# Engine order in the mixers of a two-layer hybrid encoder, and VectorE instead of GpSimd for the first weight's low half

## The chip, the cores and the metric

The kernel runs on one core of a Trainium2 chip. The metric is device time in microseconds for one launch, the median of the runs; lower is better. Engines are named as in the profile: PE is TensorE's matmul stream and PEld its weight loads, DVE is VectorE, ACT ScalarE, POOL GpSimd, SP SyncE, whose queue issues most DMAs here.

## What is computed

The input x is 512 x 1024 in fp32, the whole trunk is fp32, and the output must agree with an fp32 reference:

```python
for layer in range(2):
    h = rmsnorm(x, norm_mix[layer])
    if layer % 2 == 0:   # DeltaNet (4 heads of 128, both directions) | dilated windows (8 heads of 64)
        mixed = mixer_ab(h, ab_w_in, conv_w, a_log, dt_bias, norm_w, ab_w_out)
    else:                # retention (4 heads) | Hyena (long convolution through an FFT)
        mixed = mixer_cd(h, cd_w_in, log_decay, ..., cd_w_out)
    x = x + mixed
    x = x + conv_ffn(rmsnorm(x, norm_ffn[layer]), ffn_w_in, ffn_conv_w, ffn_conv_b, ffn_w_out)
return rmsnorm(x, final_norm)
# in DeltaNet: beta = sigmoid(b); g = -exp(a_log) * softplus(a + dt_bias)
#   sol = triangular_solve(I + strict(k_beta k^T * decay), [v * beta, k_beta * exp(g)])
```

## The kernel before

**Projections.** Every big product is done as three matmuls in a reduced fp32 format: each operand is split into a high and a low half (`whi`, `wlo`, `hh`, `hl`, ...), and `mm3` (L262 to L267) adds high by high, high by low and low by high. `fetch` (L240) takes a loaded weight block `raw` (128 x 1024 numbers, three buffers), lets ScalarE write `whi` (L253) and VectorE write `wlo` = raw - whi (L254). With `pool_lo` set, GpSimd does L254 instead. `get(ahead)` fetches until `ahead` blocks are ready and hands out the oldest; four ready blocks have room (`WB`). Activations are split in the same way by `split` (L225 on ScalarE, L226 on VectorE).

**What sets the order.** Each engine works through its own queue in order. In `start` (L189) the order is that of the program (`manual_schedule`). Everywhere else a list scheduler at build time orders each queue: by its own cost model it picks, of what it believes to be ready, what stands first in the program. `tc.issue_after(ins)` adds one constraint: what is traced in the block on `ins`'s engine comes behind `ins` in that queue; other engines are not bound by it.

**Start.** The four row tiles of x are squared and summed (L128, ScalarE), the power is taken on GpSimd (L129, L130), `scale` (L139, VectorE, two halves of a tile) multiplies by it and by the norm's row, and `turn` (L152 and the split) transposes to `hh` and `hl`. Tiles 0 and 1 come first, with the first weight block between; then tiles 2 and 3 with a block each. `first` (L278) then projects three column blocks, first over tiles 0 and 1, then over 2 and 3. `pool_lo` stays set after `start`, so the fourth block, fetched in `first`, has its low half made by GpSimd in either kernel.

**Layer 0, dilated attention, gates, DeltaNet.** `dilated` runs 16 units (scores, softmax, transposes `tp` copied to `pT` at L539, product `op` at L548), three deep. At the units named in `DPROJ` it also projects, and the last two entries call the generator `gates`: at the first it multiplies out the gate columns, at the second it computes beta and g in some 20 small operations on VectorE and ScalarE (L618 to L653), Exp at L631 and L639, Ln at L634 and L642. The third call comes in the first tile of `delta_prep` and holds the cumulative sums (`gp`, L659). `delta_prep` projects q, k and v (`tile`, each with the short convolution `conv3`, whose two VectorE steps L366 and L367 read and then release the projection's accumulator), and the gate Z (`proj_tok`). `deltanet` then inverts the triangular blocks: `Bt` is transposed (L851), 30 rank-one steps follow on VectorE (L858, L859), two transposes (L864, L865), products of 32 x 32 blocks `m32` (L890) copied to `T32` (L892), diagonal copies into P (L895), products `m32b` (L900) copied into P (L902), then the same with 64 x 64 blocks (`vp` L912, copies L913, L921, L923, L930, L932), and last a scan over four chunks. Eight units of the output projection (`fill`, 12 matmuls `oacc` each) are strewn between by `FILLS` to give PE work; `wb` are their four weight blocks.

**Layer 1.** `retention` projects q and k in four column blocks (three in `first`, one as `rqk`). Each is moved out of its accumulator by ScalarE (`rope_in`, L458), half-rotated by four DMAs (L460) and finished in `rope_out` (L467 to L478), with ScalarE casts at L474. The accumulators are then taken by `proj_tok` (`pt`). `hyena` projects 12 column blocks `hap`; after the eighth-part `HT` of the matmuls of a block it transposes u (`tp`, L1240).

Of the kernel before, what the change touches and what calls it, by code (L numbers as in the profile page):

```python
# [15 lines left out]
S = 512  # L16
# [47 lines left out]
def bc(ap, shape):  # L64
    return ap.to_broadcast(shape)
# [97 lines left out]
class K:  # L163
# [26 lines left out]
    def start(self, n):  # L190

        self.x = self.new_x()
        for what in (0, 1, None, None, 2, None, 3):
            self.load_w() if what is None else self.load_x(what)
        n.spread()
        self.warm_up(WARM)
        n.whole(0)
        n.scale(0)
        n.whole(1)
        n.scale(1)  # L200
        self.pool_lo = True
        self.fetch()
        self.pool_lo = False
        for g in range(2):
            for t in range(2):
                n.turn(t, (g,))
        for t in range(2, 4):
            self.fetch()
            n.whole(t)
            n.scale(t)  # L210
        self.pool_lo = True
# [146 lines left out]
    def conv3(self, out, ps, w, o, b=None):  # L358

        nc = self.nc  # L360
        w0, w1, w2 = [w[:, k:k + 1] for k in o]
        if b is None:
            nc.scalar.activation(out, ps, AF.Copy, scale=w1)
        else:
            nc.scalar.activation(out, ps, AF.Identity, scale=w1, bias=b)
        nc.vector.scalar_tensor_tensor(out[:, 1:], ps[:, :S - 1], w0, out[:, 1:], op0=ALU.mult, op1=ALU.add)  # L366
        nc.vector.scalar_tensor_tensor(out[:, :S - 1], ps[:, 1:], w2, out[:, :S - 1], op0=ALU.mult, op1=ALU.add)  # L367

# [233 lines left out]
    def gates(self, dp, n):  # L602
# [29 lines left out]
        V.tensor_scalar(e, e, 1.0, None, op0=ALU.add)  # L632
        nl = T("gnl")
        nc.scalar.activation(nl, e, AF.Ln)  # L634
        V.reciprocal(beta, e)
        V.tensor_tensor(y, gt[:, :, 8:16], bc(row[:, 0:1, :], [128, 4, 8]), op=ALU.add)
        V.tensor_scalar(u, y, -1.0, None, op0=ALU.mult)
        V.tensor_tensor(u, u, y, op=ALU.min)
        nc.scalar.activation(e, u, AF.Exp)  # L639
        nc.scalar.activation(row[:, 1, :], row[:, 1, :], AF.Exp)  # L640
        V.tensor_scalar(u, e, 1.0, None, op0=ALU.add)
        nc.scalar.activation(g, u, AF.Ln)  # L642
        V.tensor_scalar(u, u, -1.0, None, op0=ALU.add)
        V.tensor_scalar(g2, u, 0.0, None, op0=ALU.is_equal)
# [7 lines left out]
        V.tensor_tensor(g, g, y, op=ALU.add)  # L652
        V.scalar_tensor_tensor(g, g, -1.0, bc(row[:, 1:2, :], [128, 4, 8]), op0=ALU.mult, op1=ALU.mult)  # L653
        yield
        gp = self.wk((128, 128), "gp")
# [48 lines left out]
    def delta_prep(self, dp, n, gates, K_, Q_, V_, Z_):  # L704
# [24 lines left out]
        def tile(which, h):  # L729
            f = which * 4 + h  # L730
            ap = self.acc(nm="ap")
            self.last_ap = self.proj_t(self.get(), n, ap).ins
            next(gates, None)
            c = self.vscr.pop(0) if which == 2 else self.s2("c")
            self.conv3(c, ap, cw, (f, 12 + f, 24 + f))
            if which < 2 or h == 0:
                nc.scalar.activation(c, c, AF.Silu)
            pend.append((c, which, h))
# [26 lines left out]
    def deltanet(self, n, gates, yb, nxt):  # L765
        nc, I = self.nc, self.I
        V = nc.vector
        with ExitStack() as ctx:
# [81 lines left out]
            Xf = X.rearrange("p a b -> p (a b)")  # L850
            V.transpose(Xf, Bt.rearrange("p m s -> p s m"))  # L851
            tm = dp.tile([128, 256], F32, name="tm")
# [14 lines left out]
            for t in range(NT):  # L867
                self.load_x(t)
            wb = [self.get() for _ in range(4)]
            units = [(t, half) for half in range(2) for t in range(NT)]  # L870
# [17 lines left out]
            for m in range(16):  # L888
                for (d, s, o), p in zip(pairs, ps):
                    nc.tensor.matmul(p[blk(o), m, :], P[d][blk(s), m, blk(o)], Yv[d][blk(s), :, 16 * d + m], start=True, stop=True, tile_position=(32 * s, 32 * o))  # L890
            for i, ((d, s, o), p) in enumerate(zip(pairs, ps)):
                (V.tensor_copy if i % 2 else nc.scalar.copy)(T32[blk(o)], p[blk(o)])  # L892
            for q in range(4):
                for d in range(2):
                    (V.tensor_copy, nc.scalar.copy)[d](P[d][blk(q), :, blk(q)], Yu[d][blk(q), :, 16 * d:16 * d + 16].rearrange("p a m -> p m a"))  # L895
            fill(FILLS[1])
            ps = [self.wk((128, 16, 32), "m32b") for _ in pairs]
            for m in range(16):
                for (d, s, o), p in zip(pairs, ps):
                    nc.tensor.matmul(p[blk(s), m, :], T32[blk(o), m, :], Yu[d][blk(o), :, 16 * d + m], start=True, stop=True, tile_position=(32 * o, 32 * s))  # L900
            for i, ((d, s, o), p) in enumerate(zip(pairs, ps)):
                (V.tensor_copy if i % 2 else nc.scalar.copy)(P[d][blk(s), :, blk(o)], p[blk(s)])  # L902
            fill(FILLS[2])
# [124 lines left out]
    def retention(self, n, order):  # L1028
        nc, I = self.nc, self.I
        V = nc.vector  # L1030
        with ExitStack() as ctx:
# [12 lines left out]
            for i in range(4):  # L1044
                if i == 3:
                    self.proj_t(self.get(), n, ps[3])
                rin.append(self.rope_in(rp, ps[i], 1.0 if i // 2 else 0.125, self.rope_room() if i % 2 else None))
                if i < 2:
                    rot(i)
            with self.tc.issue_after(rin[3][2].ins):  # L1050
                rot(2)
                rot(3)
            v = rp.tile([128, NT, 512], F32, name="rv")
# [278 lines left out]
TPD = lambda k: k.acc  # L1332
DPROJ = (0, 2, 5, 8, 10, 15)
DAT = (1, 2)
# [5 lines left out]
IA = 3  # L1340
HT = 6
HSKIP = (1, 3)
# [58 lines left out]
```

## Time and profile before

| | |
|---|---|
| median of 3 runs | 1330.83 us (1330.3 to 1331.14) |
| the profiled execution | 1330.02 us, its span 1328.2 us |
| PE busy | 1304.8 us, 98% of the span |
| DVE, ACT, POOL busy | 750.6, 531.6, 147.4 us |
| mean granted TensorE clock | 0.996 |
| DMA | 123.61 MB, 31.2% of the 16 engines' time |

The page is read from the top: a busy time near the span names the engine that sets the end, and what that engine waits for (the waits, by who ended them) is what an edit can win. Where it is busy all the time but at a lower granted clock, the stretch table (busy time by engine, granted clock, DMA) shows it. The timelines give start, duration, engine, line, operation and, in brackets, how long the engine had stood idle and who ended that.

### The profile page before, as it was taken

How to read it: one execution, taken by the hardware profiler on the slowest of the kernel's cores; microseconds unless marked ns; L12 is line 12 of the kernel's file. 1: busy time of each engine (PE TensorE's matmuls, PEld its weight loads, DVE VectorE, ACT ScalarE, POOL GpSimd, SP SyncE). 2: the span in 40 equal slices, each digit the busy share in tenths (PEclk: the TensorE clock that was granted, in tenths of full speed). 3: DMA queues.
4: the chain of work that ended last, by engine and by line, in shares of the span. 5: the costliest groups of instructions: out<-in, count | busy, mean ns of one | idle time of the engine just before them, and what ended most of it. 6: DMA issues, size and time to landing. Idle time of an engine off the chain costs nothing.

```text
span 1328.2 us, 17628 instructions
## 1 busy us (share of the span) xinstructions
PE 1304.8 (98%) x6977; PEld 1093.2 (82%) x6977; DVE 750.6 (57%) x1085; ACT 531.6 (40%) x840; POOL 147.4 (11%) x176
## 2 busy tenths in 40 slices
PE   7999999999999999999999999999999999999997
PEld 6877788878988888888889787888898888888886
DVE  6777559957754433444436837869754442244432
ACT  4566648344433331233326424442443331133332
POOL 3354120003000000000001200124100000000002
PEclk9999999989999999999999999999999999999999
DMA  7531113411333333333323513330243333333321
GB/s 219 129 94 36 51 32 96 143 49 60 93 113 96 95 95 95 96 95 97 98 91 101 162 48 92 102 94 18 67 140 95 95 95 96 87 117 98 95 79 64
DMA packets 161025, 123.61 MB, mean 93 GB/s; under 512 B 6985, under 2 KB 134477, under 8 KB 160944
## 3 DMA queue, kind: packets, MB, share of 16 engines
q1 hardware_dynamic: 160798, 122.43, 31.2%
q8 instruction: 55, 0.90, 0.3%
q14 instruction: 26, 0.21, 0.1%
q10 hardware_dynamic: 146, 0.07, 0.0%
HBM read 117.23 MB, written 2.10 MB: 90 GB/s over the span
## 4 chain that ended last, share of the span: by engine, by line
PE 84%; DVE 7%; ACT 4%; issue 2%; DMA 1%; POOL 1%; SPq 0%; POOLq 0%; ACTq 0%; DVEq 0%
PE gup L266 11%; PE gup L265 11%; PE gup L267 11%; PE oacc L265 7%; PE oacc L267 7%; PE oacc L266 7%; PE hap L267 2%; PE pt L265 2%; PE hap L265 2%; PE hap L266 2%; PE pt L267 2%; PE pt L266 2%; PE ap L267 1%; PE ap L265 1%; PE ap L266 1%
## 5 line engine op out<-in xcount | busy, mean ns | idle before, releaser
L254 DVE TENSOR_TENSOR wlo<-raw,whi 128x1024 fp32r<-128x1024 f32 x191 | 236.0, 1237 | 304.1 <-ACT whi L253 299.3
L253 ACT CAST whi<-raw 128x1024 fp32r<-128x1024 f32 (+1 forms) x197 | 206.7, 1050 | 427.6 <-PE gup L266 186.8
L265 PE MATMUL gup<-hh,whi 128*128 128x512 f32 x656 | 255.2, 389 | 0.0
L266 PE MATMUL gup<-hl,whi 128*128 128x512 f32 x656 | 255.2, 389 | 0.0
L267 PE MATMUL gup<-hh,wlo 128*128 128x512 f32 x656 | 255.2, 389 | 0.0
L267 PEld LDWEIGHTS gup<-hh,wlo 128*128 128x128 f32 x656 | 123.1, 188 | 25.6
L265 PEld LDWEIGHTS gup<-hh,whi 128*128 128x128 f32 x656 | 123.2, 188 | 25.6
L266 PEld LDWEIGHTS gup<-hl,whi 128*128 128x128 f32 x656 | 123.2, 188 | 25.4
L265 PE MATMUL oacc<-whi,ghi 128*128 128x512 f32 x352 | 137.1, 389 | 0.0
L267 PE MATMUL oacc<-whi,glo 128*128 128x512 f32 x352 | 137.0, 389 | 0.0
L266 PE MATMUL oacc<-wlo,ghi 128*128 128x512 f32 x352 | 136.9, 389 | 0.0
L267 PEld LDWEIGHTS oacc<-whi,glo 128*128 128x128 f32 x352 | 66.1, 188 | 13.7
L265 PEld LDWEIGHTS oacc<-whi,ghi 128*128 128x128 f32 x352 | 66.1, 188 | 13.7
L266 PEld LDWEIGHTS oacc<-wlo,ghi 128*128 128x128 f32 x352 | 66.1, 188 | 13.6
L430 DVE TENSOR_TENSOR sl<-gup,sl 128x512 f32<-128x512 f32 x42 | 29.0, 692 | 81.8 <-PE gup L267 81.8
L315 DVE TENSOR_TENSOR x<-oacc,x 128x512 f32<-128x512 f32 x64 | 43.4, 685 | 49.3 <-PE oacc L267 49.2
L429 ACT ACTIVATE sl<-c 128x512 f32<-128x512 f32 x44 | 27.8, 632 | 89.2 <-DVE c L367 89.2
L265 PE MATMUL first<-hh,whi 128*128 128x256 f32 x192 | 54.9, 288 | 0.0
L266 PE MATMUL first<-hl,whi 128*128 128x256 f32 x192 | 54.5, 284 | 0.2 <-DVE hl L226 0.2
L267 PE MATMUL first<-hh,wlo 128*128 128x256 f32 x192 | 54.3, 283 | 0.0
L265 PE MATMUL pt<-whi,hh 128*128 128x512 f32 x128 | 50.2, 392 | 2.6 <-ACT room L458 1.7
L104 POOL TENSOR_SCALAR ss<-ss 128x1 f32<-128x1 f32 x16 | 5.0, 312 | 429.3 <-ACT jk L102 429.3
(422 smaller groups left out, 2346.4 us busy)
## 6 DMA issues: line engine op xcount, KB each, us to landing
raw<-in_ffn_w_in_dram SPq DMA_DIRECT2D x88, 512.0 KB, 3.8
raw<-in_ffn_w_out_dram SPq DMA_DIRECT2D x44, 512.0 KB, 3.9
raw<-in_ab_w_in_dram SPq DMA_DIRECT2D x28, 512.0 KB, 3.9
raw<-in_cd_w_in_dram SPq DMA_DIRECT2D x24, 512.0 KB, 4.3
x<-in_x_dram SPq DMA_DIRECT2D x16, 256.0 KB, 5.0
raw<-in_ab_w_out_dram SPq DMA_DIRECT2D x8, 512.0 KB, 3.8
raw<-in_cd_w_out_dram SPq DMA_DIRECT2D x8, 512.0 KB, 3.8
rs<-rt SPq DMA_DIRECT2D x32, 64.0 KB, 2.0
```

What stands on the lines that cost most here:

```text
L104: nc.gpsimd.tensor_scalar(ss[:, 1:2], ss[:, 0:1], s, EPS, op0=ALU.add, op1=ALU.add)
L253: self.nc.scalar.copy(hi, raw)
L254: (self.nc.gpsimd if self.pool_lo else self.nc.vector).tensor_tensor(lo, raw, hi, op=ALU.subtract)
L265: mm(out, a[0], b[0], start=start, stop=False)
L266: mm(out, a[0], b[1], start=False, stop=False)
L267: return mm(out, a[1], b[0], start=False, stop=stop)
L315: self.nc.vector.tensor_add(xs, acc, xs)
L429: nc.scalar.activation(sl, c, AF.Silu)
L430: nc.vector.tensor_mul(sl, up, sl)
```

## The change

There are seven edits. (1) In `start` the first block's low half is made by VectorE, in its program place behind the scaling of tile 1. (2) In `gates` the Ln for the key gate works on a copy and stands behind the other Ln, the second call comes at unit 18 rather than 15, and there is one more empty stop before the cumulative sums, so that these come a projection tile later. (3) `conv3` returns its last instruction, and the transpose L851 is queued behind that of the last tile. (4) The last of the four `get` calls for `wb` fetches nothing ahead. (5) The diagonal copies into P are queued behind the `T32` copies, six on VectorE and two on ScalarE rather than four and four, and two blocks are fetched behind the `m32b` copies. (6) In `retention` `rope_out` of block 1 is traced behind block 3's `rope_in`, its ScalarE part queued behind that. (7) `HT` goes from 6 to 7.

```diff
@@ start
-        self.pool_lo = True
         self.fetch()
-        self.pool_lo = False
@@ conv3
-        nc.vector.scalar_tensor_tensor(out[:, :S - 1], ps[:, 1:], w2, out[:, :S - 1], op0=ALU.mult, op1=ALU.add)
+        return nc.vector.scalar_tensor_tensor(out[:, :S - 1], ps[:, 1:], w2, out[:, :S - 1], op0=ALU.mult, op1=ALU.add)
@@ gates
-        nl = T("gnl")
-        nc.scalar.activation(nl, e, AF.Ln)
         V.reciprocal(beta, e)
 ...
         V.tensor_tensor(u, u, y, op=ALU.min)
+        nl = T("gnl")
+        V.tensor_copy(nl, e)
         nc.scalar.activation(e, u, AF.Exp)
         nc.scalar.activation(row[:, 1, :], row[:, 1, :], AF.Exp)
         V.tensor_scalar(u, e, 1.0, None, op0=ALU.add)
         nc.scalar.activation(g, u, AF.Ln)
+        nc.scalar.activation(nl, nl, AF.Ln)
 ...
+        yield
         yield
         gp = self.wk((128, 128), "gp")
@@ delta_prep
-            self.conv3(c, ap, cw, (f, 12 + f, 24 + f))
+            self.last_conv = self.conv3(c, ap, cw, (f, 12 + f, 24 + f)).ins
@@ deltanet
-            V.transpose(Xf, Bt.rearrange("p m s -> p s m"))
+            with self.tc.issue_after(self.last_conv):
+                V.transpose(Xf, Bt.rearrange("p m s -> p s m"))
 ...
-            wb = [self.get() for _ in range(4)]
+            wb = [self.get(1 + (i < 3)) for i in range(4)]
 ...
-            for i, ((d, s, o), p) in enumerate(zip(pairs, ps)):
-                (V.tensor_copy if i % 2 else nc.scalar.copy)(T32[blk(o)], p[blk(o)])
-            for q in range(4):
-                for d in range(2):
-                    (V.tensor_copy, nc.scalar.copy)[d](P[d][blk(q), :, blk(q)], Yu[d]...)
+            out = [(V.tensor_copy if i % 2 else nc.scalar.copy)(T32[blk(o)], p[blk(o)]).ins
+                   for i, ((d, s, o), p) in enumerate(zip(pairs, ps))]
+            with self.tc.issue_after(out[2]), self.tc.issue_after(out[3]):
+                for q in range(4):
+                    for d in range(2):
+                        (nc.scalar.copy if d and q % 2 else V.tensor_copy)(P[d][blk(q), :, blk(q)], Yu[d]...)
 ...   (the m32b copies likewise become a list `out`)
+            with self.tc.issue_after(out[2]), self.tc.issue_after(out[3]):
+                for _ in range(2):
+                    self.fetch()
@@ retention
-                if i < 2:
+                if i == 0:
+                    rot(0)
+            with self.tc.issue_after(rin[3][2].ins):
+                for i in range(1, 4):
                     rot(i)
-            with self.tc.issue_after(rin[3][2].ins):
-                rot(2)
-                rot(3)
@@
-DPROJ = (0, 2, 5, 8, 10, 15)
+DPROJ = (0, 2, 5, 8, 10, 18)
-HT = 6
+HT = 7
```

## Rows read from the trace of the kernel before

**Rows 1.** Waits of PE, whole span: who, released by, total us, times, longest.

```profile
PE m32b L900 <- DVE s L892: 1.9, 2, 1.4
...
PE pt L265 <- ACT room L458: 1.7, 1, 1.7
...
PE m32b L900 <- ACT s L892: 1.2, 1, 1.2
...
PE pt L265 <- DVE scr L367: 0.9, 1, 0.9
...
PE op L548 <- ACT pT L539: 0.9, 1, 0.9
...
PE tp L1240 <- ACT hsh L225: 0.6, 1, 0.6
```

**Rows 2.** Timeline of the start, 8 to 28 us: start, us, engine, line, operation, [idle].

```profile
8.29 1.41 DVE L139 SCALAR_TENSOR_TENSOR xn<-x,ss,nrow 128x512 f32<-128x512 f32 x2
...
10.08 2.35 POOL L254 TENSOR_TENSOR wlo<-raw,whi 128x1024 fp32r<-128x1024 f32 x1
...
10.16 3.48 DVE L139 SCALAR_TENSOR_TENSOR xn<-x,ss,nrow 128x512 f32<-128x512 f32 x2 [0.46 <-POOL ss L130]
...
13.03 2.82 PE L152 MATMUL nt<-ident,xn 128*128 128x128 f32 x12 [2.83 <-DVE xn L139]
...
14.80 0.69 DVE L226 TENSOR_TENSOR hl<-nt,hh 128x512 fp32r<-128x512 f32 x1 [0.56 <-ACT hh L225]
...
15.87 0.41 PE L266 MATMUL first<-hl,whi 128*128 128x256 f32 x1
...
16.24 0.28 PE L265 MATMUL first<-hh,whi 128*128 128x256 f32 x1
...
22.48 3.54 DVE L139 SCALAR_TENSOR_TENSOR xn<-x,ss,nrow 128x512 f32<-128x512 f32 x2 [0.46 <-POOL ss L130]
...
27.87 0.39 PE L266 MATMUL first<-hl,whi 128*128 128x256 f32 x1 [0.21 <-DVE hl L226]
```

**Rows 3.** Timeline of ACT at the end of the dilated units, 134 to 138 us.

```profile
134.39 1.28 ACT L634 ACT_TABLE_LOAD   x1
...
137.36 0.57 ACT L539 COPY pT<-tp 128x512 f32<-128x512 f32 x1
...
137.94 1.28 ACT L642 ACT_TABLE_LOAD   x1
```

**Rows 4.** Timeline of DVE at the end of the projections, 228 to 232 us.

```profile
228.91 2.06 DVE L851 STREAM_TRANSPOSE L<-Bt 128x1024 f32<-128x1024 f32 x1
...
230.90 0.71 DVE L367 SCALAR_TENSOR_TENSOR scr<-ap,dncw,scr 128x511 f32<-128x511 f32 x1
```

**Rows 5.** Timeline of DVE in the block inverse, 262 to 276 us.

```profile
262.43 1.21 DVE L865 STREAM_TRANSPOSE vs<-L 128x1024 f32<-128x1024 f32 x1
...
266.02 1.28 DVE L251 SCALAR_TENSOR_TENSOR wlo<-raw,dnw,whi 128x1024 fp32r<-128x1024 f32 x1 [0.71 <-ACT whi L250]
...
267.92 1.26 DVE L895 COPY P<-vs 32x512 f32<-32x512 f32 x2
...
271.12 1.42 DVE L892 COPY s<-m 32x512 f32<-32x512 f32 x2
...
274.58 1.42 DVE L902 COPY P<-m32b 32x512 f32<-32x512 f32 x2 [1.32 <-PE m32b L900]
```

**Rows 6.** Timeline of ACT and of PE there: first `T32` copies, output unit.

```profile
269.52 1.18 ACT L892 COPY s<-m 32x512 f32<-32x512 f32 x2
...
265.90 0.50 PE L265 MATMUL oacc<-whi,yh 128*128 128x512 f32 x1
```

**Rows 7.** Stretches: width, busy us by engine (instructions), PEclk, DMA share, GB/s.

```profile
235.00:264.00 29.00, 29.00 (x133) 23.73 (x132) 27.45 (x62) 6.91 (x10) 1.04 (x1) 1.00 0.47 155
...
272.17:279.00 6.83, 6.41 (x147) 4.67 (x148) 2.53 (x5) 1.54 (x4) 1.04 (x1) 0.50 0.47 156
```

**Rows 8.** Timeline of ACT in retention, around 740 us.

```profile
740.18 0.60 ACT L458 ACTIVATE room<-rqk 128x512 f32<-128x512 f32 x1
```

More of the change, by code (lines that the diff above doesn't have):

```diff
@@ L890, in deltanet @@
                     nc.tensor.matmul(p[blk(o), m, :], P[d][blk(s), m, blk(o)], Yv[d][blk(s), :, 16 * d + m], start=True, stop=True, tile_position=(32 * s, 32 * o))
-            for i, ((d, s, o), p) in enumerate(zip(pairs, ps)):
-                (V.tensor_copy if i % 2 else nc.scalar.copy)(T32[blk(o)], p[blk(o)])
-            for q in range(4):
-                for d in range(2):
-                    (V.tensor_copy, nc.scalar.copy)[d](P[d][blk(q), :, blk(q)], Yu[d][blk(q), :, 16 * d:16 * d + 16].rearrange("p a m -> p m a"))
+            out = [(V.tensor_copy if i % 2 else nc.scalar.copy)(T32[blk(o)], p[blk(o)]).ins
[3 more added lines that the diff above has]
+                    for d in range(2):
+                        (nc.scalar.copy if d and q % 2 else V.tensor_copy)(P[d][blk(q), :, blk(q)], Yu[d][blk(q), :, 16 * d:16 * d + 16].rearrange("p a m -> p m a"))
             fill(FILLS[1])
@@ L900, in deltanet @@
                     nc.tensor.matmul(p[blk(s), m, :], T32[blk(o), m, :], Yu[d][blk(o), :, 16 * d + m], start=True, stop=True, tile_position=(32 * o, 32 * s))
-            for i, ((d, s, o), p) in enumerate(zip(pairs, ps)):
-                (V.tensor_copy if i % 2 else nc.scalar.copy)(P[d][blk(s), :, blk(o)], p[blk(s)])
+            out = [(V.tensor_copy if i % 2 else nc.scalar.copy)(P[d][blk(s), :, blk(o)], p[blk(s)]).ins
+                   for i, ((d, s, o), p) in enumerate(zip(pairs, ps))]
+            with self.tc.issue_after(out[2]), self.tc.issue_after(out[3]):
+                for _ in range(2):
+                    self.fetch()
             fill(FILLS[2])
```

## The prediction

> **What bounds the kernel now.** The page's busy times come first: PE works 1304.8 of the span's 1328.2 us, so PE sets the end; DVE, the next, works 750.6. What an edit can win lies in the 23.4 us in which PE does not work, and in stretches in which it works at the lower clock. So I read the waits of PE next. The six that the mixers' edits can touch are [rows 1]: 1.9 and 1.2 us at the block inverse (one place, two releasers), 1.7 in retention, two of 0.9 in layer 0, 0.6 in hyena, 7.2 us in all. The seventh stands in the timeline of the start: PE waits 2.83 us for the scaling of tile 1 [rows 2]. Last, the stretch table shows the one place where the clock fell inside the kernel: for 6.83 us from 272.17 PE ran at 0.50, the 1.2 GHz level, while the stretch up to 264 has 1.00, the 2.4 GHz level [rows 7]. It fell after PE had waited at the block inverse, so that place costs more than its waits. The sum is made against the profiled execution (1330.02 us, 1.8 of it outside the span); the median of the runs lies 0.8 above it, which I add at the end.
>
> **1, the start.** Two scaling steps of tile 0 take 1.41 us; those of tile 1 take 3.48, while GpSimd makes the low half from 10.08 for 2.35 us [rows 2]. The difference, 2.07 us, goes with the GpSimd operation: that ends at 12.43, and the transposes that need the first half of tile 1 start at 13.03. The Trainium skill, SBUF — State Buffer, section "Who interferes with whom", says that a VectorE operation with two SBUF inputs and a GpSimd operation that reads SBUF do not share but block each other for a whole operation; by that, too, the gain is the blocked time, and nothing changes for tile 3, whose scaling takes 3.54 us at 22.48 [rows 2] beside the fourth block's low half, which stays on GpSimd.
>
> What is added: VectorE makes the low half itself, 1.28 us if I take the scaled form [rows 5] for it, ahead of the splits in its queue. Scaling then ends at 11.6, the low half at 12.9, the first `hl` (0.69) at 13.6, the second at 14.3. Before, the second ended at 15.49 (14.80 + 0.69) after an idle 0.56 that now vanishes [rows 2]. So the projection starts 2.07 - 1.28 + 0.56 = 1.35 us earlier. Two corrections. A matmul takes 0.41 us at 15.87 and 0.28 at 16.24, two further on [rows 2], which is where the clock rises; if it rises no sooner, 1.3 us at one matmul every 0.19 are seven more at the lower level, 0.13 x 7 = 0.9 us lost. On the other side the second half of `first` begins at 27.87 on a `hl` that stands behind the scaling of tile 3 [rows 2], and this chain moves by up to 2.07, as ScalarE's splits do. Gain 1.5 us, bounds 0.4 and 2.1.
>
> **2, the gates.** Three table loads, the first at 134.39 and the last at 137.94, 1.28 us each, stand in ScalarE's queue among the last softmax copies; a `pT` copy comes at 137.36 behind two of them [rows 3], and PE waits 0.9 us for it [rows 1]. With the second call at the last unit these operations are traced behind the last product, and with both Ln together one load serves in place of three. The cover is then the first projection tile and the next, 24 matmuls each; the empty stop moves `gp` behind the second, so the chain has two tiles' time instead of one. Gain 0.9. Bounds 0.9 and -0.4: four small transposes now stand at the very end of the units, where a late copy of the gate columns would hold PE; the nearest row for such a stall is the 0.6 wait for one ScalarE copy [rows 1], of which I take most. The Trainium skill, ScalarE: Activation LUTs, "Table sets: the hidden batching unit", names a set that holds both exp and ln; by it the new order of the Ln would save no load. The three loads of the rows say that the program does not use such a set.
>
> **3, the transpose L851.** It takes 2.06 us at 228.91, in front of L367 at 230.90 [rows 4]; L367 frees the accumulator for which PE waits 0.9 us [rows 1]. Put behind, L367 comes 2 us earlier and that wait goes. But VectorE is busy 27.45 of the 29 us up to 264 [rows 7], with the steps that end in L865 at 263.64 [rows 5] and so release `m32`; swapping two of its operations does not shorten that chain. PE comes 0.9 earlier and waits there. I count nothing, bounds 0 and 0.9 (the upper, if the planner draws another output unit ahead of `m32`).
>
> **4 and 5, the block inverse.** Now both queues do diagonal copies (1.26 for two on VectorE) and two scaled splits (1.28 each on VectorE [rows 5]) before the four `T32` copies, which come at 269.52 on ScalarE [rows 6] and at 271.12 on VectorE, 1.42 for two [rows 5]. `m32` has ended by 265.90, where an output unit begins [rows 6]; the last `T32` copy ends at 272.54, and 3.1 us of PE's time before that are waits [rows 1], so the unit covers PE to about 269. After: `T32` right behind `m32`, done by 265.9 + 1.4 = 267.3, inside the unit; `m32b` can start at 269 instead of 272.5. The 3.1 us of waits go. If the clock then stays up, the 6.41 us of PE work at 0.50 [rows 7] shrink as well, by 3.2 if all of it streams, which the small products do not.
>
> Against that: VectorE has six diagonal copies (6 x 0.63 = 3.8) and some three additions of output units (0.69 each, as the `hl` step of the same size [rows 2]; 2.1) in front of its two `m32b` copies, so these end near 267.3 + 3.8 + 2.1 + 1.4 = 274.6, and `vp` needs them. `m32b` took 2.0 (272.54 to 274.58 [rows 5]) and ends at 271; one output unit of 3 us is all that PE has from there. Behind come the two splits, 2.56 on VectorE and about that on ScalarE, in front of the copies of `vp`; until now both engines had done them earlier. Before, the `m32b` copies ended at 276.0 (274.58 + 1.42). So the path is 1.4 us shorter at that point, 3.1 if the planner puts those copies sooner, and part of the 3.2 of the clock comes on top. I take 2.9, nearer to the upper of these two than to the sum of everything. Bounds 0.5 (the splits take the rest) and 6.3 (3.1 + 3.2).
>
> **6, retention.** `rqk` is moved out at 740.18 [rows 8], behind the casts of block 1 in ScalarE's queue, and PE waits 1.7 us for its accumulator [rows 1]. The copy takes 0.60 and its input is ready before block 1's casts are; queued first it needs to come only 1.7 sooner. What it delays are casts whose readers come after the four weight blocks of `pt`. Gain 1.7, bounds 0.8 (it still stands behind the casts of block 0 and a split) and 1.7.
>
> **7, hyena.** The transposes of u stand three matmuls later, each at least 0.19 after the one before (those of 256 columns, [rows 2]; these have 512), and the wait was 0.6 [rows 1]. Gain 0.6, bounds 0 (the last u's splits then reach the forward transform later) and 0.6.
>
> **The sum.** 1.5 + 0.9 + 0 + 2.9 + 1.7 + 0.6 = 7.6 us: 1330.0 - 7.6 = 1322.4 for a profiled execution, 1323.2 for the median. Low bounds: 0.4 - 0.4 + 0 + 0.5 + 0.8 + 0 = 1.3; high: 2.1 + 0.9 + 0.9 + 6.3 + 1.7 + 0.6 = 12.5. Neither end is likely on all seven at once, so I take 2.0 and 11.5 off the median: 1319.3 to 1328.8.
>
> **Rivals.**
> A, the wait moves on in the block inverse: PE waits for `vp`'s copies behind the two splits, the clock falls as before, and edits 3 to 5 bring nothing. For it: one unit of 3 us must cover 3.6 (271 to 274.6) and the splits. Against: 3.1 us of wait go at the outset. Time: 1323.2 + 2.9 = 1326.1.
> B, PE's gains are waited away in layer 0: chains on VectorE and ScalarE set the pace there, and what the start and edits 2 to 5 give is given back; retention and hyena stay. Time: 1330.8 - 2.3 = 1328.5, no change by measure. For it: VectorE hardly pauses before 264 [rows 7]. Against: these chains begin on what PE delivers, so they move with it.
> C, the order does not come out as meant: the planner goes by its own times, and nothing binds VectorE in edit 6 or ScalarE in edit 2. Then a wait of about the same size stands beside each: about 1330.
> D, slower: PE's idle time at `vp` (A's wait, with no unit left) drops the clock, and the scan behind, made of short products with waits between, does not bring it back at once. The price: a microsecond of PE's work at 1.00 costs up to one more at 0.50 [rows 7]. It outweighs the remaining 4.7 us of gain and the 2.7 that count from 7.4 us of such work, a little more than the 6.41 that it was before, on top of these; over three such stretches the end would be near 1326.1 + 3 x 6.4 = 1345. Against: before, the clock was back after 6.83 us [rows 7].
> E, one set of tables serves Exp and Ln: edit 2 is only a move, and its 0.9 is lost if ScalarE delays the first tiles: 1324.1.
>
> **How the numbers follow.** Forecast 0.60, A 0.20, B 0.08, C 0.05, D 0.05, E 0.02. The range from 1319.3 to 1328.8 holds the forecast but for its tails, A, E and part of B. A measurement of this kernel tells a change of about 0.2%, 2.7 us, from none: below 1328.2 is faster. The forecast, A, E and a little of B make 0.85; the rest of B, and C, 0.10; D 0.05.
>
> **What would show it.** Start: tile 1's scaling at 1.4 us instead of 3.48, the first `hl` matmul near 14.6. Gates: one table load for Ln, no wait of `op` on `pT`. L851 behind L367, PE's 0.9 gone, and in its place a wait of `m32` for L865. Block inverse: `T32` between 266 and 268 (less what came before), no wait of `m32b`, 1.00 there. Retention: the copy of `rqk` ahead of block 1's casts. I am wrong if PE waits for `vp`'s copies longer than 3 us, if the stretch at 0.50 is as long as before, or if a new wait above 1 us stands in the softmax units.

## The result and the profile after

The changed kernel takes 1319.69 us (median of 5 runs, 1319.62 to 1320.09), the kernel before beside it 1330.83 (5 runs): ratio 0.9913, 95% interval 0.9900 to 0.9927. The medians lie 11.1 us apart, 0.8 to 0.9%. The forecast was 1323.2, so the direction is right, but the gain is 3.5 us, nearly half, larger than the sum made it: the time stands on the low end of the range (1319.3), 0.4 above it by the median and just under it by the ratio (0.9913 of 1330.83 is 1319.25).

The profiled execution took 1319.69 us, 1317.9 of it in the span. The page's busy times and its row of the granted clock:

```profile
PE 1302.9 (99%) x6977; PEld 1092.6 (83%) x6977; DVE 750.7 (57%) x1089; ACT 526.9 (40%) x837; POOL 144.4 (11%) x175
...
PEclk9999999999999999999999999999999999999999
```

PE's busy time fell by 1.9 us (from 1304.8), its idle time by 8.4 (from 23.4 to 15.0). So some of the gain is work that runs faster, not only waits that went. What is left of PE's waits (who, released by, total us, times, longest):

```profile
PE nrowp L91 <- DMA nrow<-in_norm_mix_dram: 3.8, 1, 3.8
PE nt L152 <- DVE xn L139: 0.8, 1, 0.8
...
PE m L891 <- DVE vs L866: 0.4, 1, 0.4
...
PE vp L917 <- DVE P L903: 0.2, 1, 0.2
PE tp L1245 <- ACT hsh L223: 0.2, 1, 0.2
```

Against [rows 1]: both waits of `m32b`, that for `room`, that for `scr` and that of `op` are gone; `tp` for `hsh` fell from 0.6 to 0.2. New are 0.4 at `m` (the `m32` products), 0.2 at `vp` for the `m32b` copies, and 0.2 at a product of hyena's (`hm`) for a weight transfer. The wait of `nt` fell from 2.83 to 0.8. The 3.8 at `nrowp`, for the first transfer, no edit touches.

**The start**, against [rows 2] (timeline: start, us, engine, line, operation, [idle before, and what ended it]):

```profile
10.03 1.41 DVE L139 SCALAR_TENSOR_TENSOR xn<-x,ss,nrow 128x512 f32<-128x512 f32 x2 [0.46 <-POOL ss L130]
...
10.84 2.82 PE L152 MATMUL nt<-ident,xn 128*128 128x128 f32 x12 [0.76 <-DVE xn L139]
...
11.37 1.21 DVE L252 TENSOR_TENSOR wlo<-raw,whi 128x1024 fp32r<-128x1024 f32 x1
...
12.50 2.51 DVE L224 TENSOR_TENSOR hl<-nt,hh 128x512 fp32r<-128x512 f32 x4
...
13.83 0.38 PE L264 MATMUL first<-hl,whi 128*128 128x256 f32 x1
...
14.05 0.28 PE L265 MATMUL first<-hh,wlo 128*128 128x256 f32 x1
...
20.28 3.54 DVE L139 SCALAR_TENSOR_TENSOR xn<-x,ss,nrow 128x512 f32<-128x512 f32 x2 [0.45 <-POOL ss L130]
```

Tile 1 is scaled in 1.41 us, not 3.48. The twelve transposes start at 10.84, not 13.03: 2.19 earlier. The low half (11.37 to 12.58) lies beside them. Tile 3 is stretched as before.

**The gates**, against [rows 3] (timeline of ACT): the last `pT` copy comes first, the copy of the gate columns after it, and one table load serves both Ln.

```profile
133.06 0.59 ACT L537 COPY pT<-tp 128x512 f32<-128x512 f32 x1 [1.46 <-PE tp L535]
...
135.83 0.22 ACT L622 COPY gt<-bat 128x64 f32<-128x64 f32 x1
...
138.30 1.28 ACT L641 ACT_TABLE_LOAD   x1
```

**The transpose of L**, against [rows 4] (DVE): the order is turned round.

```profile
226.33 0.74 DVE L365 SCALAR_TENSOR_TENSOR scr<-ap,dncw,scr 128x511 f32<-128x511 f32 x1
226.99 2.07 DVE L852 STREAM_TRANSPOSE L<-Bt 128x1024 f32<-128x1024 f32 x1
```

**The block inverse**, against [rows 5, 6]. DVE, then ACT at the end of it:

```profile
259.94 1.85 DVE L313 TENSOR_TENSOR x<-oacc,x 128x512 f32<-128x512 f32 x3
262.12 1.42 DVE L892 COPY s<-m 32x512 f32<-32x512 f32 x2 [0.34 <-PE m L891]
...
267.16 0.69 DVE L313 TENSOR_TENSOR x<-oacc,x 128x512 f32<-128x512 f32 x1
267.88 1.42 DVE L903 COPY P<-m32b 32x512 f32<-32x512 f32 x2
269.80 0.42 DVE L918 COPY s<-vp 64x256 f32<-64x256 f32 x1 [0.50 <-PE vp L917]
270.25 2.48 DVE L249 SCALAR_TENSOR_TENSOR wlo<-raw,dnw,whi 128x1024 fp32r<-128x1024 f32 x2
...
268.25 2.19 ACT L248 ACTIVATE whi<-raw,dnw 128x1024 fp32r<-128x1024 f32 x2
```

`T32` (L892) comes as soon as `m32` ends, three of the output additions (L313) stand ahead of it, one behind it, and the two splits' low halves (L249) come after the first copy of `vp`.

What this is worth is read best from one stretch, from the start of the `m32` products that read `vs` to the first `m64b` product, in both kernels. Before (stretch: width, busy us by engine PE, PEld, DVE, ACT, POOL, PEclk, DMA share, GB/s):

```profile
263.97:283.96 19.99, 16.72 (x379) 12.81 (x378) 12.68 (x20) 10.35 (x15) 1.04 (x1) 0.83 0.26 81
```

and after:

```profile
260.16:276.00 15.84, 15.64 (x374) 12.24 (x375) 13.94 (x22) 8.60 (x13) 1.04 (x1) 1.00 0.27 89
```

19.99 became 15.84, 4.15 us less. PE's idle time fell from 3.27 to 0.20 (3.07), and nearly the same products took 15.64 instead of 16.72 us (1.08), at a clock of 1.00 instead of 0.83. The stretch at 0.50 of [rows 7] does not exist any more.

**Retention**, against [rows 8] (ACT): `rqk` comes ahead of block 1's casts, though still behind block 0's and a split.

```profile
727.36 1.26 ACT L472 CAST r<-rt 64x512 fp32r<-64x512 f32 x2 [2.48 <-DVE rt L467]
728.65 1.05 ACT L251 CAST whi<-raw 128x1024 fp32r<-128x1024 f32 x1
729.60 0.59 ACT L456 ACTIVATE room<-rqk 128x512 f32<-128x512 f32 x1
730.78 1.26 ACT L472 CAST r<-room 64x512 fp32r<-64x512 f32 x2 [0.58 <-DVE room L467]
```

### The profile page after: what moved, and what is told of

The parts are those of the page before. It is cut to its first block, busy times and chain, and to the rows that moved or that the text cites. A ratio compares the mean times of both kernels' runs of the same rounds, so it can differ in the third digit from the quotient of the medians.

```text
span 1317.9 us, 17629 instructions
## 1 busy us (share of the span) xinstructions
PE 1302.9 (99%) x6977; PEld 1092.6 (83%) x6977; DVE 750.7 (57%) x1089; ACT 526.9 (40%) x837; POOL 144.4 (11%) x175
## 4 chain that ended last, share of the span: by engine, by line
PE 87%; DVE 7%; ACT 2%; DMA 1%; issue 1%; SPq 1%; POOL 1%; POOLq 0%; ACTq 0%; DVEq 0%
PE gup L264 11%; PE gup L265 11%; PE gup L263 11%; PE oacc L264 7%; PE oacc L265 7%; PE oacc L263 7%; PE pt L263 2%; PE pt L264 2%; PE pt L265 2%; PE first L264 2%; PE first L265 2%; PE first L263 2%; PE ap L263 1%; PE ap L264 1%; PE ap L265 1%; PE hap L263 1%
## 5 line engine op out<-in xcount | busy, mean ns | idle before, releaser
L313 DVE TENSOR_TENSOR x<-oacc,x 128x512 f32<-128x512 f32 x64 | 43.2, 684 | 48.6 <-PE oacc L265 48.6
```

The costliest lines, as they stand in the source:

```text
L313: self.nc.vector.tensor_add(xs, acc, xs)
```

## The experiments

All start from the changed kernel and undo one thing, or add one. They ran in three groups, each beside the kernel before (medians 1329.96, 1330.56 and 1330.85), so times compare by their ratios. Tenths of a microsecond I read elsewhere: how much later the same matmul starts in one trace than in that of the changed kernel. The columns are places: the end of the start's projection, the tiles behind the gates, the last projection tile, the stage behind `m32`, the first `m64b`, `pt` in retention, and layer 1.

```
us later than in
changed kernel      26.6  160.2  228.2  263.1  277.0  740.1   1300
before              2.19   3.74   4.54   3.82   7.98   9.96  10.34
u_start             2.55   2.56   2.50   2.47   2.47   2.44   2.19
u_gates             0.75   2.21   2.11   2.06   2.06   2.02   1.90
u_call              0.12   1.09      -      -      -   1.00   0.81
u_ln                0.55   1.11      -      -      -   1.19   0.97
u_L                 0.93   1.04   1.91   1.21   1.29   1.29   1.08
u_diag              0.27   0.27   0.26   0.22   0.73   0.72   0.72
u_fetch            -0.02  -0.02  -0.15  -0.13   3.05   3.03   3.08
u_block             0.30   0.32   0.23   0.19   4.31   4.55   4.34
u_ret               0.69      -      -      -      -   3.21   2.98
u_ht                0.52      -      -      -      -   0.57   0.85
p_lo4               0.52   0.55   0.49   0.45   0.47   0.49   0.33
ctl (unchanged)     0.06   0.08   0.03   0.00   0.00  -0.02  -0.06
```

The first column needs a word. Kernels with the same start as the changed one differ there by up to 0.93 us. The first product itself stands up to 0.28 us later, and the clock rises at a different moment in each execution: 0.7 us after the first product of `first` in the profiled runs of before and of the changed kernel, up to 3.0 us after it in others. Each product of 256 columns takes 0.41 us until then and 0.28 after. What an edit costs is therefore read from the step between two columns of its row. Each row is one execution, so a cost that changes between executions shows in it only once.

Between 740.1 and 1300, most rows shrink by 0.1 to 0.25 us. The control, u_diag and u_fetch do not, and of all fourteen traces only these three and the changed kernel's have the 0.2 us of wait at `hm`; in the rows of before and u_ht their own wait of 0.6 in hyena hides it. So up to 0.2 us of what an edit gains is waited away there.

**u_start: the low half on GpSimd again.**

```diff
         n.scale(1)
+        self.pool_lo = True
         self.fetch()
+        self.pool_lo = False
```

> The changed kernel with edit 1 undone: GpSimd makes the first block's low half again. Theory (the start's gain is the time for which the GpSimd operation holds up tile 1's scaling, all of it handed on): 2.1 us slower than the changed kernel's 1319.7, about 1321.8; scaling of tile 1 at 3.5 us again, every later PE step 2.0 to 2.2 later. Rival (the projection's start moves by 1.3 only, as the forecast's sum of queue times said, and the rest of what the traces show is a later rise of the clock in that one run): about 1321.0, and the half-clock stretch of the start as long as in the kernel before only by chance.

Measured: 1322.35 us (1321.95 to 1322.51), ratio 0.9938 (0.9926 to 0.9951). In its trace, the scaling of tile 1 and the transposes:

```profile
10.33 3.48 DVE L139 SCALAR_TENSOR_TENSOR xn<-x,ss,nrow 128x512 f32<-128x512 f32 x2 [0.46 <-POOL ss L130]
...
13.20 2.82 PE L152 MATMUL nt<-ident,xn 128*128 128x128 f32 x12 [2.83 <-DVE xn L139]
```

The block is back with the same length, and so is the wait of 2.83 us. PE stands 2.2 to 2.55 us later from there to the end of the program. About 0.5 of the 2.55 belongs to the clock, which rose 2.2 us after the first product here: p_lo4 and u_ht, with the changed kernel's start and a rise 2.3 and 2.4 us after it, stand 0.52 later. That leaves 2.0 for the edit, beside 2.19 in the row of before, whose clock rose as early as the changed kernel's. The theory held, and the rival's 1.3 did not.

**p_lo4: the fourth block's low half by VectorE too** (one line less, `self.pool_lo = True` behind the last tile's scaling is taken out).

> Everything as in the changed kernel, and the low half of the fourth block at the start is made by VectorE too, so GpSimd makes none there. Theory (the same block as that of tile 1 stretches tile 3's scaling from 1.4 to 3.54 us): tile 3's scaling takes 1.4 us, the second half of the first projection starts 0.2 to 0.8 us earlier, what its waits are worth, and the time falls by that. Rival 1 (the wait is for ScalarE's splits and PE has other work): no change. Rival 2: the 1.2 us that VectorE now spends on the low half delays its splits, and the second half starts later by up to 0.5 us.

Measured: 1320.14 us (1319.45 to 1320.26), ratio 0.9919 (0.9906 to 0.9933); the control with nothing changed, beside it, 0.9919. Tile 3's scaling and what PE then waits for:

```profile
20.41 1.41 DVE L139 SCALAR_TENSOR_TENSOR xn<-x,ss,nrow 128x512 f32<-128x512 f32 x2 [0.46 <-POOL ss L130]
...
25.47 0.63 PE L262 MATMUL first<-hh,whi 128*128 128x256 f32 x3 [0.24 <-ACT hh L222]
```

The second collision is the same effect (3.54 falls to 1.41), and no gain from undoing it shows. In neither trace does PE wait at that tile's transposes (the group of eight starts at 23.31 us in the changed kernel, at 24.19 here, where the clock had risen later); behind them it waits 0.2 us in both, here for ScalarE's cast, there for `hl`. u_ht, which keeps the collision and whose clock rose at nearly the same moment, has PE within 0.02 us of this trace at the transposes, behind them and at 26.6. The first rival held. The cost of a block is the wait behind it, not its length. What the second block costs when the clock rises as early as in the changed kernel's profile, and PE comes there 0.9 us sooner, no run shows.

**ctl: nothing changed.**

> The changed kernel once more, as the yardstick of this group. Both theories: 0.991 of the kernel before, about 1319 us. If the start's clock rises at another moment than in the first profile (13.7 us), all later work should stand later by less than 1 us, and no wait should differ.

1319.88 us (1319.41 to 1320.57), ratio 0.9919 (0.9905 to 0.9932). Its clock rose 0.6 us later than in the first profile, and PE stands within 0.1 us of it at every place behind the start.

**u_gates: the Ln order and the call's place as before.**

```diff
         V.tensor_scalar(e, e, 1.0, None, op0=ALU.add)
+        nl = T("gnl")
+        nc.scalar.activation(nl, e, AF.Ln)
...
-        nl = T("gnl")
-        V.tensor_copy(nl, e)
         nc.scalar.activation(e, u, AF.Exp)
...
-        nc.scalar.activation(nl, nl, AF.Ln)
...
-        yield
         yield
...
-DPROJ = (0, 2, 5, 8, 10, 18)
+DPROJ = (0, 2, 5, 8, 10, 15)
```

> The changed kernel with edit 2 undone whole (old order of the Ln, second call at unit 15, one stop fewer). Theory (what the wait of 0.9 showed is not all: products that PE had begun ran slower beside it): 1.4 us slower, about 1321.1, PE waits 0.9 for a pT copy and the 16 products behind take 1.4 instead of 1.1 us. Rival (only the listed wait): 0.9 slower, 1320.6.

Measured: 1321.43 us (1320.95 to 1321.85), ratio 0.9932 (0.9919 to 0.9944). The step in its row is 2.21 - 0.75 = 1.46 us, the same as that of the kernel before (3.74, and 2.28 at 126 us, ahead of the gates). The theory held. PE in this trace:

```profile
134.44 1.09 PE L546 MATMUL op<-pT,dv 128*64 128x128 f32 x16
136.45 1.42 PE L546 MATMUL op<-pT,dv 128*64 128x128 f32 x16 [0.91 <-ACT pT L537]
```

The listed wait is 0.91 of the step; the rest can be counted in the rows. Sixteen products by themselves take 1.09 us, the last 32 of the changed kernel, in one row, 1.97: in a running stream sixteen cost only 0.88, since a product starts before the profile ends the one ahead of it. A stop loses that 0.21 beside its listed wait. The sixteen behind it took 1.42, which is 0.33 more. Together that is 1.45. The clock rose late, in the middle of the projection:

```profile
16.16 0.38 PE L265 MATMUL first<-hh,wlo 128*128 128x256 f32 x1
16.37 0.28 PE L263 MATMUL first<-hh,whi 128*128 128x256 f32 x1
```

while in the changed kernel's profile the products are at 0.28 from 14.05. That is the 0.75 in its first column, with no edit behind it.

**u_call: only the call's place and the added stop undone** (the last two hunks above).

> Everything as in the changed kernel, but the gates are called at the old place and without the added stop; the order of the two Ln stays new. Theory (the table loads stand among the softmax copies because of the call's place): a wait of op for pT is back, of at most one table load's length, 0.3 to 0.9 us, with 1.1 to 1.45 us in PE's positions. Rival (only the number of table loads matters): one Ln load as in the changed kernel, no wait for pT, PE within 0.2 us of the changed kernel.

Measured: 1320.91 us (1320.45 to 1321.53), ratio 0.9929 (0.9916 to 0.9941). ACT:

```profile
133.59 1.28 ACT L641 ACT_TABLE_LOAD   x1
...
135.02 0.57 ACT L537 COPY pT<-tp 128x512 f32<-128x512 f32 x1
```

A single load, now ahead of the last `pT` copy, holds PE for 0.72 us (`op` for `pT`); the step is 1.09 - 0.12 = 0.97. The 0.72 and the 0.21 of lost overlap make 0.93 of it; the sixteen products behind this wait take 1.09, no longer than those ahead. The mechanism of the theory held, with a step a little under its lower number.

**u_ln: only the order of the Ln undone** (the first three hunks).

> Everything as in the changed kernel, but the first Ln stands before the second Exp again; the call's new place stays. Theory (the call's place is what counts, the loads are hidden behind two projection tiles): three table loads of 1.28 us instead of one, and PE within 0.3 us of the changed kernel. Rival (the loads delay ScalarE's copies for the next tiles): PE 0.5 to 1.5 us later. By the skill's statement that one table set holds Exp and Ln there would be no load more than in the changed kernel.

Measured: 1320.87 us (1320.32 to 1321.22), ratio 0.9928 (0.9915 to 0.9940). ACT:

```profile
138.04 1.28 ACT L632 ACT_TABLE_LOAD   x1
...
139.58 1.28 ACT L637 ACT_TABLE_LOAD   x1
...
141.12 1.28 ACT L640 ACT_TABLE_LOAD   x1
```

Three loads instead of one, 2.56 us more on ScalarE, cost PE 0.46 to 0.56 us (0.55 to 1.11 in the row; a wait of `tp` for `scr` of 0.2 appears behind the first tiles). It lies between theory and rival. The place and the order together make 0.97 + 0.5 = 1.5, the whole edit. The Trainium skill, ScalarE: Activation LUTs, "Table sets: the hidden batching unit", names a set with both functions; by it u_ln would have one load, and the trace, with three, does not agree.

**u_L: the transpose of L in front of the last convolution step** (`if True:` in place of `with self.tc.issue_after(self.last_conv):`).

> Everything as in the changed kernel, but the transpose of line 852 stands in front of line 365 again. Theory (VectorE's chain to m32 sets the pace, the swap only moves a wait): PE waits 0.9 us for pt again and that much less at m32; the scan begins within 0.2 us of where it does in the changed kernel, time the same within 0.3 us. Rival (the 0.8 us gained at pt is kept): 0.8 us longer.

Measured: 1320.74 us (1320.13 to 1321.05), ratio 0.9924 (0.9910 to 0.9937), beside the control's 0.9919. PE's wait there:

```profile
PE pt L263 <- DVE scr L365: 1.0, 1, 1.0
```

The row shows the exchange: 0.87 us later at 228.2 (1.91 - 1.04), 0.70 of it got back by 263.1, because the 0.4 at `m` goes. At the first `m64b` 0.25 is left (1.29 - 1.04); behind it the row shrinks by 0.2 as others do. The theory held, slightly past its 0.2.

**u_diag: the diagonal copies not bound behind T32, four on each engine; the splits stay late.**

```diff
-            with self.tc.issue_after(out[2]), self.tc.issue_after(out[3]):
+            if True:
                 for q in range(4):
                     for d in range(2):
-                        (nc.scalar.copy if d and q % 2 else V.tensor_copy)(P[d]...
+                        (V.tensor_copy, nc.scalar.copy)[d](P[d]...
```

> The changed kernel with the first half of edit 5 undone: diagonal copies four and four, not bound behind the T32 copies; the two fetches stay behind the m32b copies. Theory (the T32 copies behind the diagonal ones are the cause of the wait and of the fall of the clock): m32b waits 2 to 3 us, the clock falls to 0.50 for some 7 us, about 3.5 us slower, 1323.2. Rival (the two splits in front of T32 were the cause, and they are gone from there): T32 comes at most 1 us later, the unit covers it, the clock stays, less than 1 us slower, 1320.2.

Measured: 1320.72 us (1320.51 to 1321.6), ratio 0.9928 (0.9915 to 0.9941). `T32` and PE's wait for it:

```profile
264.56 1.42 DVE L892 COPY s<-m 32x512 f32<-32x512 f32 x2
...
PE m32b L902 <- DVE s L892: 0.4, 1, 0.4
```

`T32` is 2.4 us later than in the changed kernel, and PE waits only 0.4, since the output unit covers the rest. The clock stays at 1.00. The step is 0.5 us. So the theory fell and the rival held in the time, though `T32` came later than the rival's 1 us.

**u_fetch: the two splits early again, with four plain fetches; the diagonal copies stay bound.**

```diff
-            wb = [self.get(1 + (i < 3)) for i in range(4)]
+            wb = [self.get() for _ in range(4)]
...
-            with self.tc.issue_after(out[2]), self.tc.issue_after(out[3]):
-                for _ in range(2):
-                    self.fetch()
```

> The changed kernel with edit 4 and the second half of edit 5 undone: the last wb call fetches one block ahead, and the two scaled blocks are fetched where the scheduler likes. Theory (the binding of the diagonal copies is what counts; the splits fill gaps wherever they stand): within 1 us of the changed kernel, 1319.7 to 1320.7, T32 within 1 us of m32's end. Rival (a scaled split of 1.28 on VectorE and its half on ScalarE in front of T32 bring back a wait of m32b and the fall of the clock): 2 to 3 us slower, about 1322.2.

Measured: 1324.04 us (1323.01 to 1324.8), ratio 0.9951 (0.9937 to 0.9966). DVE, PE's wait, and the stretch behind it:

```profile
260.38 1.27 DVE L249 SCALAR_TENSOR_TENSOR wlo<-raw,dnw,whi 128x1024 fp32r<-128x1024 f32 x1
...
262.16 1.28 DVE L249 SCALAR_TENSOR_TENSOR wlo<-raw,dnw,whi 128x1024 fp32r<-128x1024 f32 x1
...
264.07 1.42 DVE L892 COPY s<-m 32x512 f32<-32x512 f32 x2
...
270.64 1.42 DVE L903 COPY P<-m32b 32x512 f32<-32x512 f32 x2
...
PE vp L914 <- DVE P L903: 2.5, 1, 2.5
...
273.26:276.67 3.41, 3.41 (x58) 3.17 (x54) 1.14 (x4) 0.82 (x2) 0.00 (x0) 0.50 0.00 0
```

The two splits stand ahead of `T32`, and all that follows on VectorE is late by their length: the `m32b` copies start 2.76 us later than in the changed kernel (270.64 against 267.88), PE waits 2.5 us for them, and the clock falls to 0.50 for 3.41 us. The step is 3.2 us in all (-0.13 to 3.05). The theory fell and the rival held, with the wait at `vp` and not at `m32b`. It is close to rival A of the prediction, a wait at `vp` and a fall of the clock; only it comes about when the splits are not moved. The profiled execution (1323.12) is one of the two shortest of the five: by the medians u_fetch costs 4.2 to 4.4 us (1324.04 against 1319.88 and 1319.69), so the 3.2 is a low value.

**u_block: both parts undone.**

> Everything as in the changed kernel, but both parts of the block inverse's order are undone: the diagonal copies are not bound behind the T32 copies, and the two splits come early. Theory (the two parts act on one queue and add up to what the block gained): PE waits about 3 us for m32b again, the clock falls to 0.50 for about 6.8 us, and the scan begins 4.1 us later than in the changed kernel, about 1323 us beside it. Rival (the splits' place alone is the whole of it, the diagonal copies hide anyway): like the kernel with the early splits alone, 3.0 us later, with the wait at vp and not at m32b.

Measured: 1324.4 us (1323.87 to 1326.57), ratio 0.9955 (0.9943 to 0.9967). PE's waits:

```profile
PE m32b L902 <- DVE s L892: 1.9, 2, 1.5
PE m32b L902 <- ACT s L892: 1.4, 1, 1.4
```

Those are the waits of [rows 1], to 0.2 us, and the step is 4.1 us (0.19 to 4.31), the whole of the block's gain. Alone the parts cost 0.5 and 3.2 in these traces; together 4.1. The theory held, and the rival, that the copies' place has no part in it, did not.

**u_ret: the rotations in the old order.**

```diff
-                if i == 0:
-                    rot(0)
-            with self.tc.issue_after(rin[3][2].ins):
-                for i in range(1, 4):
+                if i < 2:
                     rot(i)
+            with self.tc.issue_after(rin[3][2].ins):
+                rot(2)
+                rot(3)
```

> Everything as in the changed kernel, but retention draws the rotations in the old order (two, then the rest behind the last input). Theory (the copy of rqk queued behind the casts is the whole of the 1.85 us by which PE's work moved there): the wait of about 1.7 us for its accumulator is back, PE stands 1.85 us later from there to the end, about 1321.7 beside 1319.9. Rival (part of it is kept because the block of weights stands differently): less than 1.2 us.

Measured: 1322.64 us (1322.15 to 1323.15), ratio 0.9941 (0.9929 to 0.9954). It is more than expected: a step of 2.6 us at `pt` (0.63 to 3.21), 2.3 at the end, with a wait of 2.3 where before has 1.7. The theory's cause held, its size did not. What fits the excess stands 20 us earlier, on ACT:

```profile
712.17 1.98 ACT L1067 ACTIVATE gen<-rel,ld 128x896 f32<-128x896 f32 x2 [0.75 <-DMA ld<-in_ret_log_decay_dram]
...
PE pt L263 <- ACT room L456: 2.3, 1, 2.3
```

ScalarE waited 0.75 us for a small transfer, where in the profile of before it waited 0.16: 0.59 more, as PE's wait is 0.6 longer. The landing varies: 0 to 0.86 us of wait in the fourteen profiles. In the old order, of which there are these two traces only, PE pays for it, since ScalarE's chain sets the release of the accumulator. In the new one it has slack: u_ln waits 0.80 there,

```profile
712.60 1.98 ACT L1066 ACTIVATE gen<-rel,ld 128x896 f32<-128x896 f32 x2 [0.80 <-DMA ld<-in_ret_log_decay_dram]
```

and PE has no wait at `pt` behind it, only 0.19 us more in its row (1.00 at the end of layer 0, 1.19 at `pt`).

**u_ht: `HT = 6` again.**

> Everything as in the changed kernel, but in hyena the transposes of u stand one step earlier again. Theory: the wait for ScalarE's split (0.6 us in the kernel before, 0.18 in the changed one) is back and PE stands 0.4 to 0.6 us later behind it, at the end too; in the time about 0.5 us, at the edge of what it can tell. Rival (given back in the transform behind it): no difference at the end.

Measured: 1320.17 us (1320.11 to 1320.59), ratio 0.9923 (0.9910 to 0.9937). The wait is back:

```profile
PE tp L1245 <- ACT hsh L223: 0.6, 1, 0.6
```

and the step is 0.3 us (0.57 to 0.85) at the end. That is under the theory's 0.4, and not a full giving back; the 0.2 at `hm` is absent here. No time of this kernel could tell it; the positions do.

## What the prediction had right, and the terms of its sum that failed

Order, mechanisms and signs came out as the profile of before had shown them. The sum of 7.6 us was too small. The step that failed most is the term of the block inverse: it was held down to 2.9 us because VectorE's queue ahead of `vp` was thought full, and 4.2 came. The start (0.7 short), the gates (0.6) and the 0.8 added for the median follow. That the range nearly held the time is partly luck: start, gates and retention came out at or above their own upper bounds (2.1, 0.9 and 1.7), and only the unused part of the block's bound of 6.3 made up for it. The terms beside the steps of before's row, which by construction add up to the 10.34 at its end:

```
                          forecast   measured
start                          1.5        2.2
gates                          0.9        1.5
transpose of L                 0.0        0.1
block inverse                  2.9        4.2
retention                      1.7        2.0
hyena and the rest             0.6        0.4
offset of the median          (0.8)       0.0
```

**The start: 1.5 said, 2.2 came.** The price of the block, 2.07 us, was right: 3.48 became 1.41, and the whole excess went. Two steps of the working failed. First, the low half's 1.28 was put on the path. It lies beside the twelve transposes of PE, which take 2.82 us [rows 2] and in which PE has nothing to wait for; the first `hl` product came 2.04 us earlier (15.87 to 13.83). The cover was in the rows that were read, and the sum did not name it. Second, the correction of 0.9 us for a clock that rises no sooner. In the two profiles it rose 0.7 us after the first product, so none of it was due. That is chance: in other executions with the changed start it rose up to 3.0 us after it (u_gates, u_L), near the 16.2 us of before, and PE then stood 0.75 to 0.93 later. The working of the 0.9 was also too high: it took 0.13 us a product from the listed lengths, while the starts of these products lie 0.21 us apart at the lower level (u_gates) and 0.12 at the higher. With the clock alike the gain is 2.0 to 2.2, and the upper bound, 2.1, was the right value. The statement that tile 3's stretch stays and changes nothing held, and p_lo4 shows why.

**The gates: 0.9 said, 1.5 came.** Place and table loads did what was written: one load for Ln, no wait of `op`. The term was the listed wait, and that was taken as the upper bound. u_call and u_ln give 1.0 and 0.5; a wait of 0.7 went with 1.0 of time. A stop also loses the overlap of the products on both sides of it, 0.2 us here, and in u_gates the products behind it ran 0.3 longer; no list of waits counts either. Rival E falls with u_ln: without the new order there are three loads.

**The transpose: nothing said, 0.1 came** (0.25 by u_L). The exchange is as written: 0.8 us gained at `pt`, 0.7 of it waited away at `m32`, where 0.4 of wait is new.

**The block inverse: 2.9 said, 4.2 came.** This is the step that failed. The two parts of the gain were both priced: 3.1 of waits, of which 3.07 went, and up to 3.2 of the clock, of which 1.08 came. What failed is the deduction between. `T32` ended where it was put, at 263.5, which is 267.3 in before's time. The `m32b` copies were to end near 274.6 for lack of room on VectorE, and ended at 269.3, which in before's time (3.8 later) is 273.1: 1.5 us sooner. Three output additions (2.1 us) were counted between `T32` and those copies, and one stood there; three ran before `T32`, while VectorE waited for `m32` anyway. And the splits were booked as a cost, in front of `vp`'s copies. On VectorE they came behind the first of these, where it has time: PE's list has no wait for a copy of `vp`. By the rows of u_fetch and u_diag their move is 3.2 of the block's 4.2 us, the diagonal copies' place 0.5 of it alone. The sum entered the move only through the earlier `T32`, and then filled the room that it leaves between `m32` and `vp` with work that was not there. What is like rival A comes without that move. One reading was off, without harm: the `m32b` products of before did not all start behind the last `T32` copy at 272.54, the first stood at 270.15; the 2.0 us taken for them is what they took in the changed kernel (265.02 to 267.02). Rival D did not come: with 0.2 us of wait at `vp` the clock stays at 1.00.

**Retention: 1.7 said, 2.0 came**, the listed wait and a little more, and more still where the small transfer lands late (2.3 to 2.6 in u_ret).

**Hyena: 0.6 said, 0.3 to 0.4 came**; 0.2 of the wait is left, and 0.2 is new at `hm`.

**The offset.** 0.8 us were added because the median of before lay that much over its profiled run. The changed kernel's median equals its profiled run. The record says where before's spread comes from. Of its 27 runs beside the experiments (1328.66 to 1333.1) the five shortest, up to 1329.01, all have a mean granted clock of 0.998, and the seven longest, from 1332.26, have 0.994 or 0.995. The changed kernel and its control (1319.41 to 1320.57) have 0.998 or 0.999. So before's time at the lower clock differs from run to run, and the kernel without a fall inside spreads by 1.2 us. That the 0.8 is part of this is argued, not shown; and the 4.2 of the block is the value of one execution of before, whose clock fell for 6.83 us.

Rival B fell: nothing of what the start, the gates or the block gained was lost behind them, as the rows of u_start, u_gates and u_block show, which change by 0.4 at most from there to the end. Rival C fell by the order in the timelines.

## What to carry to other kernels

Price an added operation by the engine that has to wait for it, and look for what PE does in that time: the low half of 1.2 us was free beside 2.8 us of transposes, and undoing the second collision, just as long as the first, showed no gain. When work is moved, enter both ends: what its old place gets rid of (here 2.5 us ahead of a chain that PE waits for) as well as what its new place has to bear. And a listed wait is no upper bound for what goes with it: the lost overlap of the products around it (0.2 to 0.5 us at the gates), the clock behind it (1.1 in the block inverse) and a transfer that lands later (0.6 in u_ret) came on top.

## What the runs showed of the hardware that was not expected

- The moment of the clock's first rise varies between executions of the same start: 0.7 to 3.0 us after the first projection product in the fourteen profiles. With the up to 0.28 us by which the first product varies, it moves the rest of the program by up to 0.93 us (u_L against the changed kernel).
- A wait of 2.5 us at `vp` (u_fetch) was followed by a fall to 0.50 for 3.41 us, one of 0.4 us at `m32b` (u_diag) by none. The length of one wait alone does not tell: in before the two that ended ahead of the fall at 272.17 were 1.2 and 1.4 [rows 1], and one of 2.3 us at `pt` in retention (u_ret) was followed by no fall; the granted clock there is 1.00 from 700 to 800 us.
- The block of VectorE's scaling by a GpSimd low half has the same length wherever it stands: 3.48 for tile 1 (before and u_start) and 3.54 for tile 3, for two steps that take 1.41 alone. The Trainium skill, SBUF — State Buffer, section "Who interferes with whom", describes it as an exclusive lock and not a sharing. The traces agree for VectorE, the engine that was held: its excess of 2.07 and 2.13 us is most of GpSimd's 2.35 and 2.41, and all of it falls on the first of the two steps (2.82 and 2.88 us, the second 0.74).
- A transfer of 4 KB at retention was awaited from 0 to 0.86 us in profiles of nearly the same program.
